# Other priorities in the first stage of a transformer-trunk kernel: gating columns ahead of a latent block, gate products and norm statistics first on VectorE

## The chip, the cores and the metric

The kernel runs on one core of one Trainium2 chip. The metric is the device time of one execution in microseconds (us); the time given is the median of some runs. In the profile PE is the tensor engine (PEld its weight loads, which overlap), DVE is VectorE, ACT is ScalarE, POOL is GpSimd, SP is SyncE, which issues most DMAs here.

## What is computed

One layer of a decoder trunk over 1024 tokens of width 1024, in float32. The input is RMS-normalized and multiplied by one input projection, whose columns feed four groups of heads; each group's output (width 256) is RMS-normalized, and all go through one output projection and are added to the residual. A squared-ReLU MLP of width 4096 and a last RMSNorm follow.

```
z = rms_norm(h, mix_norm_g[l]) @ w_in[l]
z_conv, z_mla, z_pool, z_gmlp = jnp.split(z, split_at, axis=-1)
...
# conv_module: y = a * sigmoid(g); causal depthwise convolution with 31 taps;
y = jax.nn.silu(layer_norm(y, ln_g, ln_b))
return y @ pw_w
...
# spatial_gating: v = rms_norm(v); chunks of 128 tokens, 4 heads
gate = jnp.einsum('hij,bnjhd->bnihd', ws * causal, v) + bs.T[None, None, :, :, None]
return u * gate.reshape(b, s, GROUP_WIDTH)
...
h = h + mixed @ w_out[l]
f = jnp.square(jax.nn.relu(rms_norm(h, ffn_norm_g[l]) @ w_ff1[l]))
h = h + f @ w_ff2[l]
```

"Latent" columns are those of the latent attention (z_mla, 352 columns), "gating" columns those of the spatial gating (z_gmlp, 512 columns).

## The kernel before

Every float32 matmul is done as three passes over a high and a low part (`mm3`, L160): ScalarE writes the rounded high part, VectorE (or GpSimd) the difference, the low part (`split`, L131 to L133; `split_scaled`, L135 to L137). Tokens are handled in two halves of 512 (`hf`) and eight tiles of 128.

The first stage, to about 400 us, holds everything up to the MLP. `z_mm(name, hf, jp)` (L421) projects the gating columns ("zgm") or the latent ones ("zml") of two token tiles: 48 matmuls into one `X` tile of PSUM (two such tiles exist), over four weight slices `zgm0` to `zgm3` or `zml0` to `zml3`. Each slice is loaded and split by `z_load`. Then the tile is read by `evac_gmlp` (ScalarE copies and squares, L441 to L443, a power on GpSimd, a scaling on VectorE, L446) or by `evac_mla` (ScalarE L457 to L459, small copies on GpSimd, scalings on VectorE, L463 and L464). `gmlp` (L501) multiplies the gating weights with the normalized half (gate matmuls, L510), then VectorE forms the products `ug` (L515: gate plus bias, times u), and PE transposes them (`ogT`, L521). The convolution (`conv_even_odd`, L353) is a chain of about 30 taps for each of two channel halves on VectorE (L351); its sum is `acc`. `conv_ln(u)` (L557) does the layer norm for a quarter of the tokens: four PE transposes into the one `K` bank of PSUM (`lnb`, L562), statistics (L567), aggregation (L568), a power on GpSimd, normalization (`yn`, L572), and four transposes back (`lnT`, L577). `wo_tile` multiplies a group's output with the output projection and adds it to the residual `h` (L495, "residual sum").

Up to the MLP the order of the work isn't written out. The kernel is traced in program order, and when it is built a planner runs through it on a clock of its own estimates: whenever an engine is free, it gives it the ready instruction with the lowest rank. The rank is the position in the program; inside `tc.high_priority(offset=n)` it is that position less n. The result is one fixed queue for each engine; on the chip each engine takes its queue in order and waits where an operand isn't there. Offsets of 2000 and 4000 reach ahead of everything that is traced up to there; an offset of 1 is nearly none. Tiles of one tag (`X`, `K`) were handed out in program order in the run before. The MLP from about 400 us on is ordered by hand (`run`, L905), and the planner doesn't touch it.

The part of the program text that the change touches stands in this order: `z_mm("zgm", 1, 0)`; `z_mm("zml", 1, 1)` at 4000; `gmlp(0)`; weights of the output projection at 300; `z_mm("zml", 0, 0)` at 2000; `z_mm("zml", 0, 1)`; `gmlp(1)`; `z_mm("zml", 1, 0)`; pooling; the convolution; `conv_ln(0)`, and between other work `conv_ln(1)` to `conv_ln(3)`.

Of the kernel before, what the change touches and what calls it, by code (L numbers as in the profile page):

```python
# [12 lines left out]
ALU = mybir.AluOpType  # L13
# [14 lines left out]
GW = 256  # L28
# [21 lines left out]
C_BS = 19  # L50
# [12 lines left out]
def trunk_kernel(tc, a):  # L63
    nc = tc.nc
    act = nc.scalar
    dve = nc.vector
    pool = nc.gpsimd
    pe = nc.tensor
    with (
        tc.tile_pool(name="sb", bufs=1) as sb,  # L70
        tc.tile_pool(name="ps", bufs=1, space=bass.MemoryType.PSUM) as ps,
        tc.tile_pool(name="hbm", bufs=1, space=bass.MemoryType.DRAM) as hbm,
    ):
        _trunk(tc, nc, act, dve, pool, pe, sb, ps, hbm, a)


def _trunk(tc, nc, act, dve, pool, pe, sb, ps, hbm, a):
# [4 lines left out]
    def const(shape, name, dt=F32):  # L82
        return sb.tile(shape, dt, tag=name, name=name)
# [6 lines left out]
    def pair(tag, name, shape):  # L90
        return [U(tag, name + "_h", shape, F32R), U(tag, name + "_l", shape, F32R)]
# [14 lines left out]
    def M(name, shape):  # L106
        return sb.tile([P] + shape, F32, tag="M", name=name, bufs=NM)
# [7 lines left out]
    def small(n, name, bufs=2):  # L115
        return sb.tile([P, n], F32, tag=name, name=name, bufs=bufs)

    def X(name):
        return ps.tile([P, 1024], F32, tag="X", name=name, bufs=2)

    def W(name):
        return ps.tile([P, 512], F32, tag="W", name=name, bufs=2)

    def K(name):
        return ps.tile([P, 512], F32, tag="K", name=name, bufs=1)

    def O(name):
        return ps.tile([P, 512], F32, tag="O", name=name, bufs=1)


    def split(h, l, src):  # L131
        act.activation(h, src, AF.Copy)
        dve.tensor_sub(l, src, h.bitcast(F32))  # L133
# [30 lines left out]
    def power(out, ssq, n, name, scale, expo):  # L164
        ms = small(n, name + "_ms")
        pool.tensor_scalar(ms, ssq, scale, EPS, ALU.mult, ALU.add)
        pool.tensor_tensor(out, ms, expo[:, :n], ALU.pow)

    def rstd(ssq, n, name, scale=1.0):
        rs = small(n, name + "_rs")  # L170
        power(rs, ssq, n, name, scale, nhalf)
        return rs


    cols = const([P, NCOL], "cols")
# [91 lines left out]
    b = X("zc")  # L267
# [56 lines left out]
    for i, hf in ((1, 0), (0, 1), (1, 1)):  # L324
        if (i, hf) == (0, 1):
            ba, bg = K("zc"), O("zc")
        else:
            b = X("zc")
# [46 lines left out]
    for i in range(2):  # L375
        w = load_w(a["w_cm"][4 + i], 1024, "wp%d" % i)
        b = X("zp")
# [43 lines left out]
    def z_mm(name, hf, jp):  # L421
        width, evac = {"zgm": (512, evac_gmlp), "zml": (352, evac_mla)}[name]
        b = X(name)
        for s in range(4):
            for j in range(2):
                lo = (2 * jp + j) * P
                for kk in range(2):
                    k = 2 * s + kk
                    mm3(b[:, j * 512:j * 512 + width], lambda x: xk(hf, k, x, lo, lo + P),
                        lambda y: wz[name, s][:, y, kk * width:(kk + 1) * width], k == 0, k == KD - 1)  # L430
        for j in range(2):
            evac(hf, 2 * jp + j, b[:, j * 512:(j + 1) * 512])
# [68 lines left out]
    def gmlp_chain(hf, wst):  # L501
        vs = pair("O", "gv", [4, GW])
        split(vs[0], vs[1], vg[hf])
        og = ug[hf]
        for hp in range(2):
            b = W("gate")
            for j in range(2):
                hd = 2 * hp + j
                for i, (x, y) in enumerate(PASSES):
                    pe.matmul(b[:, j * GW:(j + 1) * GW], wst[:, x, hd * P:(hd + 1) * P],  # L510
                              vs[y][:, :, hd * 64:(hd + 1) * 64], start=i == 0, stop=i == 2)
            for j in range(2):
                hd = 2 * hp + j
                og_h = og[:, :, hd * 64:(hd + 1) * 64]
                dve.scalar_tensor_tensor(og_h, b[:, j * GW:(j + 1) * GW].rearrange("p (n c) -> p n c", n=4),  # L515
                                         cols[:, C_BS + hd:C_BS + hd + 1], og_h, ALU.add, ALU.mult)
        oT = pair("OP"[hf], "oTg", [2, 512])
        for ct in range(2):
            b = W("ogT")
            for j in range(4):  # L520
                pe.transpose(b[:, j * P:(j + 1) * P], og[:, j, ct * P:(ct + 1) * P], ident)  # L521
            split(oT[0][:, ct, :], oT[1][:, ct, :], b)
        ssq = small(4, "ogs")
        jk = M("ogj", [GW])
        for j in range(4):
            act.activation(jk, og[:, j, :], AF.Square, accum_out=ssq[:, j:j + 1])
        return oT, rstd(ssq, 4, "ogr", 1.0 / GW)
# [29 lines left out]
    def conv_ln(u):  # L557
        hf = u // 2
        b = K("lnb")
        for j in range(2):  # L560
            for ct in range(2):
                pe.transpose(b[:, j * GW + ct * P:j * GW + (ct + 1) * P],  # L562
                             acc[ct][:, j, u * P:(u + 1) * P], ident)
        st = small(12, "bst", 1)
        mv = small(4, "bmv", 2)
        for j in range(2):
            dve.bn_stats(st[:, 6 * j:6 * j + 6], b[:, j * GW:(j + 1) * GW])  # L567
            dve.bn_aggr(mv[:, 2 * j:2 * j + 2], st[:, 6 * j:6 * j + 6])  # L568
        rs = rstd(mv.rearrange("p (j c) -> p j c", c=2)[:, :, 1], 2, "lnr")
        yn = M("yn", [2 * GW])  # L570
        for j in range(2):
            dve.tensor_scalar(yn[:, j * GW:(j + 1) * GW], b[:, j * GW:(j + 1) * GW], mv[:, 2 * j:2 * j + 1],  # L572
                              rs[:, j:j + 1], ALU.subtract, ALU.mult)
        b = O("lnT")
        for ct in range(2):
            for j in range(2):
                pe.transpose(b[:, ct * GW + j * P:ct * GW + (j + 1) * P], yn[:, j * GW + ct * P:j * GW + (ct + 1) * P],  # L577
                             ident)
        vh = M("vh", [2, GW])
        for ct in range(2):  # L580
            act.activation(vh[:, ct, :].rearrange("p (n c) -> p c n", c=2),
                           b[:, ct * GW:(ct + 1) * GW].rearrange("p (c n) -> p c n", c=2), AF.Identity, scale=lnhalf[:, ct:ct + 1],
                           bias=lnhalf[:, 2 + ct:3 + ct])
        th = M("th2", [2, GW])
        act.activation(th, vh, AF.Tanh)
        dve.scalar_tensor_tensor(vh, th, 1.0, vh, ALU.add, ALU.mult)
        if u % 2 == 0:
            us[hf] = pair("BP"[hf], "us%d" % hf, [2, 512])
        sl = slice((u % 2) * GW, (u % 2 + 1) * GW)
        split(us[hf][0][:, :, sl], us[hf][1][:, :, sl], vh)  # L590
# [713 lines left out]
    def gmlp(hf):  # L1304
        outs[3, hf] = gmlp_chain(hf, wst)
# [28 lines left out]
    with tc.high_priority(offset=1000):  # L1334
        load_wo(3, 1, pool)
    z_mm("zgm", 1, 0)
    with tc.high_priority(offset=4000):
        z_mm("zml", 1, 1)
    gmlp(0)
    with tc.high_priority(offset=300):  # L1340
# [18 lines left out]
    with tc.high_priority(offset=300):  # L1359
        wo_tile(3, 0, 3)  # L1360
        wo_tile(3, 0, 1)
    conv_ln(0)
    latent_T(0)
    with tc.high_priority(offset=300):
        load_h(4)
    outs[2, 1] = pool_chain(1, pw)
    conv_ln(1)
    wo_tile(3, 0, 0)
    load_h(5)
    load_wo(0, 1, pool)  # L1370
    wo_tile(3, 1, 1)
    conv_ln(2)
    with tc.high_priority(offset=300):
        wo_tile(2, 0, 2)
# [303 lines left out]
```

## Time and profile before

| | |
|---|---|
| median of 3 runs | 1024.47 us (1022.46 to 1025.44) |
| profiled execution | 1026.12 us, its span 1024.4 us |
| busy, PE / DVE / ACT / POOL | 993.5 / 822.5 / 500.8 / 206.1 us |
| mean granted PE clock | 0.988 |

The span is the time from the first to the last instruction of the profiled execution. In a row of the list in order of time stand start, duration, engine, line, operation, output<-inputs, shapes and count; in brackets the idle time of the engine just before, and what ended it. In a row of the list of waits stand the total, the count and the longest. In a row of the windows stand the window, its length, then each engine's busy time, the granted PE clock, and the DMAs' share and rate.

### The profile page before, as it was taken

The page shows a single profiled execution, that of the slowest core. Times are in us where ns is not written, and L with a number is a line of the kernel's source. Part 1 is how long each engine was busy: PE and PEld are TensorE (multiplying, and loading weights), DVE is VectorE, ACT ScalarE, POOL GpSimd, SP SyncE. Part 2 cuts the span into 40 slices and gives each one's busy share as a digit, 9 for nine tenths or more (in the row PEclk, how much of TensorE's full clock was granted, in tenths as well). Part 3 has the DMA queues.
Part 4 walks back from the last instruction along what each step waited for, and adds up shares of the span by engine and source line. Part 5 has one row for each costly group of instructions (what it writes and reads, how often), then busy time and mean ns, then how long its engine had stood idle before and what let it go on. Part 6 is the DMA issues. An engine that isn't in the chain of part 4 may idle for free.

```text
span 1024.4 us, 13323 instructions
## 1 busy us (share of the span) xinstructions
PE 993.5 (97%) x4674; PEld 818.5 (80%) x4674; DVE 822.5 (80%) x1275; ACT 500.8 (49%) x932; POOL 206.1 (20%) x304
## 2 busy tenths in 40 slices
PE   9999898989999999999999999999999999999996
PEld 7888697868888887878888887888688888888885
DVE  5899999977888666777776666558988888988997
ACT  7622355545667768774455554543341431431435
POOL 0037275213232312231121211211000000000004
PEclk9999999989999999999999999999999999999999
DMA  9521043011002006876766674559677067168004
GB/s 333 222 76 35 21 149 109 1 52 42 1 1 83 1 1 250 289 293 226 246 226 225 220 248 168 217 213 414 279 256 283 36 237 291 48 210 303 0 1 165
DMA packets 49348, 165.71 MB, mean 162 GB/s; under 512 B 6016, under 2 KB 7680, under 8 KB 49280
## 3 DMA queue, kind: packets, MB, share of 16 engines
q1 hardware_dynamic: 36000, 119.42, 33.2%
q0 software_dynamic: 12992, 45.10, 11.3%
q8 instruction: 37, 0.61, 0.3%
q10 hardware_dynamic: 288, 0.33, 0.1%
q14 instruction: 31, 0.25, 0.1%
HBM read 113.45 MB, written 51.38 MB: 161 GB/s over the span
## 4 chain that ended last, share of the span: by engine, by line
PE 68%; DVE 11%; issue 7%; DMA 6%; ACT 4%; POOL 3%; SPq 0%; POOLq 0%; DVEq 0%; ACTq 0%
PE ffb L162 15%; PE ffx L162 13%; PE ffa L162 11%; PE ffy L162 8%; PE wo L162 5%; PE ffe L162 4%; DVE acc L351 3%; PE ob L162 2%; PE s L698 2%; DMA raw_b<-in_w_ff 1%; DMA raw_f<-fr 1%; PE ptb L741 1%; PE woa L162 1%; DMA wcm_raw<-in_w_cm 1%; DVE h L495 1%
## 5 line engine op out<-in xcount | busy, mean ns | idle before, releaser
L162 PE MATMUL ffb<-wop,fop 128*128 128x512 f32 x756 | 179.3, 396 | 2.3 <-ACT wop L900 1.6
L162 PEld LDWEIGHTS ffb<-wop,fop 128*128 128x128 f32 x756 | 141.8, 188 | 37.7 <-ACT wop L900 2.4
L162 PE MATMUL ffx<-hnT,wop 128*128 128x512 f32 x624 | 149.5, 392 | 0.9 <-DVE s L963 0.8
L903 DVE TENSOR_TENSOR wop<-w_raw,wop 128x512 fp32r<-128x512 f32 x112 | 76.2, 689 | 78.5 <-ACT wop L900 78.3
L162 PEld LDWEIGHTS ffx<-hnT,wop 128*128 128x128 f32 x624 | 117.0, 188 | 27.7 <-DVE s L963 1.2
L162 PE MATMUL ffa<-wop,fop 128*128 128x512 f32 x576 | 135.1, 393 | 0.0
L162 PEld LDWEIGHTS ffa<-wop,fop 128*128 128x128 f32 x576 | 108.2, 188 | 25.0
L900 ACT ACTIVATE wop<-raw_b 128x512 fp32r<-128x512 f32 x96 | 59.6, 623 | 116.2 <-PE ffa L162 38.4
L900 ACT ACTIVATE wop<-w_raw 128x512 fp32r<-128x512 f32 x112 | 68.7, 625 | 42.5 <-DVE w_raw L1043 18.9
L900 ACT ACTIVATE fop<-raw_f 128x512 fp32r<-128x512 f32 x64 | 39.9, 623 | 80.2 <-DVE h_back L1099 27.6
L903 DVE TENSOR_TENSOR wop<-raw_b,wop 128x512 fp32r<-128x512 f32 x96 | 65.6, 683 | 5.8 <-ACT wop L900 5.3
L162 PE MATMUL ffe<-hnT,wop 128*128 128x512 f32 x288 | 68.7, 395 | 0.7 <-ACT m L996 0.7
L1279 POOL TENSOR_SCALAR mr_ms<-mssq,epsr 128x1 f32<-128x1 f32 x6 | 4.5, 752 | 297.4 <-ACT fjunk L1272 297.4
L162 PEld LDWEIGHTS ffe<-hnT,wop 128*128 128x128 f32 x288 | 53.5, 188 | 12.7 <-ACT m L996 1.2
L162 PE MATMUL ffy<-hnB,wop 128*128 128x512 f32 x192 | 46.9, 393 | 0.4 <-ACT s L996 0.4
L162 PE MATMUL ffy<-hnT,wop 128*128 128x512 f32 x192 | 46.5, 391 | 0.0
L974 POOL DMA_DIRECT2D fs<-fst x48 | 25.9, 539 | 90.1 <-DVE fst L133 86.7
L903 DVE TENSOR_TENSOR fop<-raw_f,fop 128x512 fp32r<-128x512 f32 x64 | 43.8, 685 | 0.0
L162 PEld LDWEIGHTS ffy<-hnB,wop 128*128 128x128 f32 x192 | 36.0, 188 | 9.0 <-ACT s L996 0.9
L162 PEld LDWEIGHTS ffy<-hnT,wop 128*128 128x128 f32 x192 | 36.1, 188 | 8.0
L721 POOL TENSOR_SCALAR P<-P,rr 128x384 f32<-128x384 f32 (+7 forms) x32 | 24.6, 768 | 47.8 <-DVE rr L720 47.5
L698 PE MATMUL s<-kb,qT 128*128 128x512 f32 (+2 forms) x144 | 32.9, 360 | 0.8 <-DVE h L495 0.8
(462 smaller groups left out, 2169.5 us busy)
## 6 DMA issues: line engine op xcount, KB each, us to landing
fs<-fst POOLq DMA_DIRECT2D x48, 512.0 KB, 3.3
fop<-fs SPq DMA_DIRECT2D x48, 512.0 KB, 7.7
w_raw<-in_w_ff SPq DMA_DIRECT2D x44, 512.0 KB, 4.3
raw_b<-in_w_ff SPq DMA_DIRECT2D x32, 512.0 KB, 5.4
raw_f<-fr SPq DMA_DIRECT2D x32, 512.0 KB, 5.3
fr<-s POOLq DMA_DIRECT2D x32, 256.0 KB, 3.2
fr<-f POOLq DMA_DIRECT2D x20, 256.0 KB, 2.4
xin<-in_x SPq DMA_DIRECT2D x8, 512.0 KB, 8.4
```

The lines of the kernel that those rows point to most:

```text
L162: pe.matmul(out, lhs(x), rhs(y), start=start and i == 0, stop=stop and i == 2, skip_group_check=more)
L351: dve.scalar_tensor_tensor(out[:, k:], src[:, 0:512 - k], c, out[:, k:], ALU.mult, ALU.add)
L495: dve.scalar_tensor_tensor(h[t], b, rs, h[t], ALU.mult, ALU.add)
L698: pe.matmul(sb_[:, c0:c0 + w], q[:, x, qo:qo + P], kt[:, y, 0:w], start=i == 0, stop=i == 2 and not last)
L721: pool.tensor_scalar(pt, pt, rr, 1.0, ALU.mult, ALU.mult)
L741: pe.transpose(b[:, place[j] + s * P:place[j] + (s + 1) * P], pts[s][:, (2 * kp + j) * P:(2 * kp + j + 1) * P], ident)
L900: act.activation(self.t[:, 0], self.src(), AF.Copy)
L903: dve.tensor_sub(self.t[:, 1], self.src(), high(self.t))
L974: pool.dma_start(fs[p][q], t.rearrange("p x c -> p (x c)").bitcast(F32))
L1279: eng.tensor_scalar(ms, fin["ssq", t], epsr[:, t:t + 1], 1.0, ALU.add, ALU.mult)
```

## The change

Three places get other priorities; no instruction is added or removed. The latent block of tiles 6 and 7 loses its offset of 4000 (1 is left), the gate products and all VectorE and GpSimd work of a norm quarter up to the normalization get 4000, and the four transposes of a norm quarter are traced with the second channel half first.

```diff
@@ gmlp_chain
             for j in range(2):
                 hd = 2 * hp + j
                 og_h = og[:, :, hd * 64:(hd + 1) * 64]
-                dve.scalar_tensor_tensor(og_h, b[:, j * GW:(j + 1) * GW].rearrange("p (n c) -> p n c", n=4),
-                                         cols[:, C_BS + hd:C_BS + hd + 1], og_h, ALU.add, ALU.mult)
+                with tc.high_priority(offset=4000):
+                    dve.scalar_tensor_tensor(og_h, b[:, j * GW:(j + 1) * GW].rearrange("p (n c) -> p n c", n=4),
+                                             cols[:, C_BS + hd:C_BS + hd + 1], og_h, ALU.add, ALU.mult)
@@ conv_ln
-        for j in range(2):
-            for ct in range(2):
+        for ct in (1, 0):
+            for j in range(2):
                 pe.transpose(b[:, j * GW + ct * P:j * GW + (ct + 1) * P],
                              acc[ct][:, j, u * P:(u + 1) * P], ident)
-        st = small(12, "bst", 1)
...
+        with tc.high_priority(offset=4000):
+            st = small(12, "bst", 1)
+            mv = small(4, "bmv", 2)
+            for j in range(2):
+                dve.bn_stats(st[:, 6 * j:6 * j + 6], b[:, j * GW:(j + 1) * GW])
+                dve.bn_aggr(mv[:, 2 * j:2 * j + 2], st[:, 6 * j:6 * j + 6])
+            rs = rstd(mv.rearrange("p (j c) -> p j c", c=2)[:, :, 1], 2, "lnr")
+            yn = M("yn", [2 * GW])
+            for j in range(2):
+                dve.tensor_scalar(yn[:, j * GW:(j + 1) * GW], b[:, j * GW:(j + 1) * GW], mv[:, 2 * j:2 * j + 1],
+                                  rs[:, j:j + 1], ALU.subtract, ALU.mult)
@@ the program text
     z_mm("zgm", 1, 0)
-    with tc.high_priority(offset=4000):
+    with tc.high_priority(offset=1):
         z_mm("zml", 1, 1)
     gmlp(0)
```

More of the change, by code (lines that the diff above doesn't have):

```diff
@@ L559, in conv_ln @@
         b = K("lnb")
-        for j in range(2):
-            for ct in range(2):
+        for ct in (1, 0):
+            for j in range(2):
                 pe.transpose(b[:, j * GW + ct * P:j * GW + (ct + 1) * P],
                              acc[ct][:, j, u * P:(u + 1) * P], ident)
-        st = small(12, "bst", 1)
[L565 to L573, printed above, removed]
+        with tc.high_priority(offset=4000):
[9 more added lines that the diff above has]
+                                  rs[:, j:j + 1], ALU.subtract, ALU.mult)
         b = O("lnT")
```

## The prediction

> **What bounds the kernel now.** I read the page first, then the list of waits for the tensor engine (PE), then a table of time windows, then the instructions in order of time around each hole. The page:
>
> ```profile
> span 1024.4 us, 13323 instructions
> PE 993.5 (97%) x4674; PEld 818.5 (80%) x4674; DVE 822.5 (80%) x1275; ACT 500.8 (49%) x932; POOL 206.1 (20%) x304
> DVE  5899999977888666777776666558988888988997
> PEclk9999999989999999999999999999999999999999
> ```
>
> PE is busy for 993.5 of 1024.4 us, so a gain can only come from the 31 us in which it is not, or from busy time at a lower clock. VectorE (DVE) has 80% over the span, but in its slices 2 to 8 (26 to 205 us) stand an 8 and six 9s: it is full in the stage that the change touches. What PE waits for, the largest rows that lie in this stage:
>
> ```profile
> PE ogT L521 <- DVE ug L515: 3.3, 2, 2.8
> PE zml L162 <- ACT zgm L443: 3.0, 1, 3.0
> PE lnT L577 <- DVE yn L572: 2.5, 1, 2.5
> PE zml L162 <- DVE zml0l L133: 0.9, 1, 0.9
> PE zml L162 <- DVE zml3l L133: 0.8, 1, 0.8
> ```
>
> These are 3.3 + 3.0 + 2.5 + 0.9 + 0.8 = 10.5 us. The windows show what comes with them (busy time of each engine, then the granted clock under PEclk):
>
> ```profile
> 75.00:164.00 89.00, 80.98 (x419) 71.20 (x418) 86.31 (x129) 35.78 (x92) 51.89 (x55) 0.97 0.24 81
> 118.30:121.60 3.30, 2.81 (x7) 2.33 (x8) 2.58 (x5) 2.16 (x4) 3.05 (x4) 0.50 0.00 0
> 123.50:159.80 36.30, 34.98 (x223) 34.32 (x224) 34.50 (x58) 18.04 (x53) 23.71 (x31) 1.00 0.45 157
> 162.70:165.90 3.20, 2.79 (x10) 2.33 (x11) 3.16 (x7) 1.89 (x4) 2.90 (x5) 0.50 0.56 172
> 220.70:234.20 13.50, 12.33 (x34) 9.37 (x35) 7.57 (x13) 6.47 (x12) 2.19 (x2) 0.50 0.00 0
> 234.80:400.00 165.20, 162.20 (x983) 139.55 (x983) 125.47 (x215) 111.10 (x221) 48.90 (x78) 1.00 0.11 35
> ```
>
> From 75 to 164 us DVE is busy for 86.31 of 89 us: there it sets the pace, and PE waits. In three places PE runs at half clock, for at least 3.3, 3.2 and 13.5 us. At full clock this work takes half as long, so the three cost about 1.6, 1.6 and up to 6.7 us. After 234.8 us PE is busy for 162.20 of 165.20 us at full clock, so there is little to win there and something to lose. The three holes, with their clock, are worth about 3.0 + 1.6, 2.8 + 1.6 and 2.5 + 6.7 = 18 us: the ceiling of the change.
>
> **The latent block moved back (4000 to 1).** No instruction is added. The 48 matmuls of this block, its reads of the bank on ScalarE, four small POOL copies, the POOL powers and four DVE scalings lose their lead; it issues no DMA, so SP's queue is passed by nothing. Around it:
>
> ```profile
> 115.35 0.40 PE L162 MATMUL zgm<-zgm3h,xT_l 128*128 128x512 f32 x1
> 118.79 0.66 PE L162 MATMUL zml<-zml0h,xT_h 128*128 128x352 f32 x1 [3.04 <-ACT zgm L443]
> ...
> 122.21 0.40 PE L162 MATMUL zgm<-zgm3h,xT_l 128*128 128x512 f32 x1
> 123.55 0.43 PE L162 MATMUL zml<-zml0l,xT_h 128*128 128x352 f32 x1 [0.95 <-DVE zml0l L133]
> ...
> 130.69 0.43 PE L162 MATMUL zml<-zml3l,xT_h 128*128 128x352 f32 x1 [0.76 <-DVE zml3l L133]
> ```
> ```profile
> 122.61 0.89 DVE L133 TENSOR_TENSOR zml0l<-zml_raw,zml0h 128x704 fp32r<-128x704 f32 x1
> ```
>
> PE's queue holds the first latent matmul ahead of the last nine gating ones. It waits 3.04 us for a bank that ScalarE still reads; then the nine run; then PE waits 0.95 us for zml0l. With the change the nine run in the hole, from 115.6 to about 117.7 (nine at the pitch of 0.23 us that the starts before the hole have). But the second latent matmul still needs zml0l, which VectorE writes at 122.61 to 123.50, behind convolution taps that this edit doesn't move. So by 123.55 PE has done exactly the same work: value 0. Two ends. Below nothing: a block of offset 2000 that follows can now overtake the moved one, and its first three quarters cover the 0.76 us before 130.69: -0.8. Above: the holes merge into one of about 5.4 us (0.9 ahead of the one latent matmul, 4.4 behind it), and by the rows above 3.04 us idle was enough for a stretch of half clock; two such stretches from 121.6 on would cost half of the 5 us that lie after 123.55, +2.5. That is less than the 2.77 us that PE idles at 163.12 below, so I keep 0.
>
> **The gate products first on DVE.** Eight instructions change rank; none is added.
>
> ```profile
> 157.01 0.28 PE L510 MATMUL gate<-gv_h,wst 128*128 128x256 f32 x1
> 163.12 1.94 PE L521 MATMUL ogT<-ident,ug 128*128 128x128 f32 x8 [2.77 <-DVE ug L515]
> ```
> ```profile
> 153.67 1.21 DVE L133 TENSOR_TENSOR gv_l<-vg,gv_h 128x1024 fp32r<-128x1024 f32 x1
> ...
> 160.25 1.28 DVE L137 SCALAR_TENSOR_TENSOR wo_0l<-wo_raw,cols,wo_0h 128x1024 fp32r<-128x1024 f32 x1
> 161.45 0.73 DVE L351 SCALAR_TENSOR_TENSOR acc<-ycv,hsum,acc 128x502 f32<-128x502 f32 x1
> 162.10 1.65 DVE L515 SCALAR_TENSOR_TENSOR ug<-gate,cols,ug 128x256 f32<-128x256 f32 x4
> ```
>
> The products (L515) start at 162.10, though the gate matmuls end at 157.29: 4.8 us that a first rank could win. But the tap just ahead (161.45) is written later in the program than the products, so it ranked lower already, and still went first. So the planner's own clock did not hold the products ready; a higher rank doesn't help an instruction that the planner thinks is not ready. Value 0; the other end is the whole hole and its half clock, -(2.8 + 1.6) = -4.4. No end above nothing: what they could push back is taps, which have slack until the first norm at 172.13. I take 0 as the nearer, by the tap at 161.45.
>
> **The norm statistics first on DVE, and the transposes' order.** Four units of two statistics, two aggregates and two normalizations on DVE and two small POOL operations move up; no DMA, so SP's queue is passed by nothing, and POOL sat idle before the small operations anyway:
>
> ```profile
> POOL lnr_ms L166 <- DVE bmv L568: 22.3, 3, 12.6
> ```
>
> The 16 transposes into the bank stay 16, in another order; both statistics start together once the bank is full (172.13), and would after: 0. First and last unit, and the cost of a projection tile:
>
> ```profile
> 172.13 0.76 DVE L567 BATCH_NORM_STATS2 bst<-lnb 128x6 f32<-128x256 f32 x2
> ...
> 178.26 0.99 DVE L572 TENSOR_SCALAR yn<-lnb,bmv,lnr_rs 128x256 f32<-128x256 f32 x2
> ...
> 216.16 0.75 DVE L137 SCALAR_TENSOR_TENSOR cT<-ctb,cols,cT 128x512 fp32r<-128x512 f32 x1
> 216.83 1.27 DVE L495 SCALAR_TENSOR_TENSOR h<-wo,cr_cr,h 128x1024 f32<-128x1024 f32 x1
> 218.02 0.75 DVE L567 BATCH_NORM_STATS2 bst<-lnb 128x6 f32<-128x256 f32 x2
> ...
> 218.77 0.66 DVE L133 TENSOR_TENSOR oTc_l<-pwc,oTc_h 128x512 fp32r<-128x512 f32 x1
> 219.35 0.17 DVE L568 BATCH_NORM_AGGREGATE bmv<-bst 128x2 f32<-128x6 f32 x1
> ...
> 220.62 1.00 DVE L572 TENSOR_SCALAR yn<-lnb,bmv,lnr_rs 128x256 f32<-128x256 f32 x2 [0.53 <-POOL lnr_rs L167]
> ```
> ```profile
> 218.30 0.39 PE L162 MATMUL pwc<-us_h,cw 128*128 128x512 f32 x1
> 221.22 1.36 PE L577 MATMUL lnT<-ident,yn 128*128 128x128 f32 x4 [2.53 <-DVE yn L572]
> ```
> ```profile
> 235.68 2.75 PE wo L162 x12
> ```
>
> In the first unit 6.1 us pass from statistics to normalization (172.13 to 178.26), with residual sums (L495) between. Rank can take out some 3 us, but PE is full of projection matmuls there: 0. In the last unit PE has nothing else: its hole from 218.69 to 221.22 is this chain. One residual sum (216.83, 1.27 us, next start 1.19 us later) goes ahead of the statistics; it is the one piece in which rank can matter. The copy at 218.77 ranked lower and still went, so it fills a gap that rank doesn't close; so does the POOL power (219.52 to 220.62). I take -1.2; the ends are 0 (the statistics were not ready either) and -2.5 (the hole goes).
>
> **The half clock behind the last norm.** With 1.2 us less the hole is 1.3 us. Nearest rows: 0.95 us (before 123.55) was followed by full clock (the window from 123.5), 2.53, 2.77 and 3.04 us by half clock. 1.3 lies nearest to 0.95, so the 13.5 us at half clock go. PE was busy for 12.33 of them, and would need 6.2; but DVE has 7.57 us of work in the same stretch, partly in line with PE, so I let it shrink to about 9: -4.5, with ends 0 and -6.2. By the Trainium skill (TensorE: Matmul & The Clock Gate, Part 1) a gate halves the clock after at least one idle window of about 3.4 us. The length of the stretches agrees (3.3, 3.2, and 13.5 as four), the threshold does not: holes of 2.5 to 3.0 us were enough here.
>
> **What can be pushed back.** Statistics (0.94 us a unit from 218.02 to about 218.96 if nothing lies between) and normalizations (0.99 us) now go ahead of residual sums. A projection tile takes PE 2.75 us, and its sum 1.27 us, in two banks: 1.5 us of cover. Should the statistics stand in DVE's queue before the bank is full, everything behind them waits too, sums and splits. Value 0; if it goes, 4 units by 0.4 us, and up to three stretches of half clock.
>
> **Sum.** 0 + 0 - 1.2 - 4.5 = -5.7 us. The profiled execution took 1026.12 us (span 1024.4 and 1.7 around it), 1.65 us more than the median of the runs, 1024.47. Against its own time that is 1020.4; against the median, 1018.8 us.
>
> **The rivals.** First, nothing that counts moves: VectorE's order is set by what the planner held ready, the last norm keeps its place, and PE's order moves with it. Speaks for it: the taps at 161.45 and the copy at 218.77, both of lower rank and both first. Against: the sum at 216.83. Time 1024.5, give or take 3. In this case the change doesn't do what it says.
>
> Second, a special form of it, on the clock. If the 13.5 us at half clock were not set off by the hole but by what PE did in them (four transposes, then matmuls with breaks), they stay when it shrinks: only -1.2, 1023.3 us. Against it: half clock follows all three holes of 2.53 to 3.04 us. The Trainium skill's page on TensorE, by the rule given above, would have it this way, since no hole here is a whole window.
>
> Third, slower: the norms come ahead of the residual sums and the banks come free late. It decides once a sum ends more than 1.5 us late, and 0.94 + 0.99 us put ahead of one sum pass that by 0.4. Four units make 1.7 us of holes, and if each of two or three brings a stretch of half clock at 1.6 us, or the one at 220.7 stays and another comes, 4 us more: about +6, 1030.5 us. The planner works every later order out anew, and the 165 us after 234.8 have only 3 us of idle to lose to, which makes new holes likelier than fewer.
>
> Fourth, faster still: the products also pass the weight split at 160.25 and the taps around it, and the second hole goes: 1018.8 - 4.4 = 1014.4 us.
>
> **How the numbers follow.** Forecast 0.36, fourth 0.11, first 0.21, second 0.05, third 0.27. Faster by over 0.3% (3.1 us, about what a measurement can tell here) is 0.36 + 0.11 = 0.47, the same 0.26, slower 0.27. The range goes from the fourth's time less some of the first edit's and the last norm's other ends (-0.8, -1.3, -1.7), 1011, to the third's, 1030. The forecast's own range is 1015 to 1021.
>
> **What would show it.** Right: a hole before lnT L577 under 1.5 us and full clock in the 15 us after it; zml0l still the wait of the first latent block, with gating matmuls ahead of its first one; products at the old distance from the gate matmuls, and the ogT hole at 2 to 3 us. Wrong: half clock after lnT as before, PE waits on residual sums L495 between 165 and 218 us, or new holes after 235 us.

## The result, and the profile after

The kernel after takes 1030.94 us (median of 4 runs, 1030.73 to 1031.68), the kernel before 1024.95 us beside it (4 runs, 1022.46 to 1026.56). The ratio is 1.0063, with a 95% interval of 1.0046 to 1.0080: the change costs some 6 us, where 5.7 us of gain were forecast. The profiled execution after took 1031.14 us.

The page of the kernel after, the lines that answer to those of before:

```profile
span 1029.4 us, 13322 instructions
PE 993.0 (96%) x4674; PEld 817.8 (79%) x4674; DVE 824.2 (80%) x1275; ACT 501.3 (49%) x932; POOL 211.1 (21%) x304
PEclk9999999999999999999999999999999999999998
```

PE is busy for 993.0 us, as before (993.5); the span is 5 us longer. So the loss is time in which PE does nothing. Where it lies is seen from the time windows of the kernel after (PE, PEld, DVE, ACT and POOL busy, then the granted clock), and for comparison those of a run that has the queues of before (e3, below):

```profile
75.00:164.00 89.00, 82.67 (x422) 73.33 (x422) 86.01 (x128) 36.58 (x98) 55.12 (x56) 0.96 0.22 76
164.00:200.00 36.00, 32.82 (x164) 26.54 (x162) 31.62 (x50) 15.17 (x30) 11.83 (x16) 1.00 0.15 50
200.00:235.00 35.00, 28.08 (x136) 22.07 (x135) 30.25 (x45) 18.83 (x32) 7.99 (x8) 0.97 0.12 38
235.00:400.00 165.00, 162.00 (x974) 139.22 (x974) 124.02 (x213) 110.35 (x219) 47.84 (x76) 1.00 0.09 28
```

```profile
75.00:164.00 89.00, 82.45 (x418) 72.14 (x416) 86.33 (x127) 35.54 (x91) 52.19 (x56) 0.96 0.23 81
164.00:200.00 36.00, 35.97 (x171) 30.07 (x171) 33.26 (x58) 18.04 (x41) 10.38 (x18) 0.91 0.10 35
200.00:235.00 35.00, 31.52 (x152) 25.24 (x151) 29.18 (x42) 19.58 (x32) 7.74 (x7) 0.95 0.11 38
235.00:400.00 165.00, 162.00 (x979) 139.24 (x978) 125.75 (x216) 111.87 (x223) 48.22 (x78) 1.00 0.12 41
```

In the stage of the edit, up to 164 us, PE is as busy as in e3, and from 235 us on the two are alike (162.00 of 165 us). From 164 to 235 us PE has 32.82 + 28.08 = 60.9 of 71 us instead of 35.97 + 31.52 = 67.5: 6.6 us of holes more. The higher clock there (1.00 and 0.97 for 0.91 and 0.95) gives back about half of that. What PE waits for from 164 to 235 us in the kernel after:

```profile
PE wo L162 <- DVE h L495: 2.1, 2, 1.6
PE wo L162 <- ACT oTp_h L136: 1.6, 1, 1.6
PE wo L162 <- DVE oTg_l L133: 1.6, 2, 1.3
PE qb L162 <- ACT vh L583: 1.2, 1, 1.2
PE ctb L611 <- DVE cT L137: 1.2, 1, 1.2
PE pwc L162 <- ACT us_h L132: 1.1, 1, 1.1
```

No wait is longer than 1.6 us. The two long ones of before in this neighbourhood, ogT (2.77 us) and lnT (2.53 us), are both gone: small waits have taken their place. The place that the edit touches, in PE's order of time:

```profile
120.66 0.43 PE L162 MATMUL zml<-zml0h,xT_h 128*128 128x352 f32 x1 [0.78 <-ACT zgm L443]
125.41 0.66 PE L162 MATMUL zml<-zml0l,xT_h 128*128 128x352 f32 x1 [4.33 <-DVE zml0l L133]
125.87 0.49 PE L162 MATMUL zml<-zml0h,xT_l 128*128 128x352 f32 x1
126.16 0.41 PE L510 MATMUL gate<-gv_h,wst 128*128 128x256 f32 x1
```

The nine gating matmuls now run ahead, and the two waits (3.04 and 0.95 us before) have become 0.78 and 4.33 us, with a single matmul between. Behind them the gate matmuls (L510) of the first half stand between the latent ones. Before, three of them came ahead of the block's last quarter (from 129.42 us) and the rest behind the block.

One more thing has to be known before any number is compared. Run e3 has every queue in the order of before, but its trace has other stretches of half clock:

```profile
119.00:125.80 6.80, 5.81 (x14) 4.41 (x15) 6.08 (x11) 2.39 (x5) 4.13 (x4) 0.50 0.07 8
163.40:170.20 6.80, 6.17 (x18) 4.96 (x19) 6.73 (x13) 5.32 (x20) 4.24 (x7) 0.50 0.34 119
224.80:228.20 3.40, 3.40 (x10) 2.30 (x9) 2.00 (x4) 2.40 (x4) 2.42 (x2) 0.51 0.00 0
```

The same three holes are followed by 6.8, 6.8 and 3.4 us at half clock here, by 3.3, 3.2 and 13.5 us in the profile shown before. Behind the last hole the stretch differs by 10 us between two executions of the same queues, which is 5 us of matmul work.

### The profile page after: what moved, and what is told of

It reads as the page before. It is cut to its first block, busy times and chain, and to the rows that moved or that the text cites. A ratio compares the mean times of both kernels' runs of the same rounds, so it can differ in the third digit from the quotient of the medians.

```text
span 1029.4 us, 13322 instructions
## 1 busy us (share of the span) xinstructions
PE 993.0 (96%) x4674; PEld 817.8 (79%) x4674; DVE 824.2 (80%) x1275; ACT 501.3 (49%) x932; POOL 211.1 (21%) x304
## 4 chain that ended last, share of the span: by engine, by line
PE 46%; issue 25%; DVE 10%; POOL 8%; DMA 6%; ACT 4%; SPq 0%; POOLq 0%; DVEq 0%; ACTq 0%
PE ffb L162 15%; PE ffa L162 11%; PE wo L162 4%; PE ffe L162 4%; DVE acc L351 3%; POOL fr L961 3%; PE ob L162 2%; PE s L700 2%; POOL fs L976 2%; DMA xraw<-in_xT 2%; DMA raw_f<-fr 2%; PE ptb L743 1%; PE woa L162 1%; DVE h L495 1%; DMA fop<-fs 1%
```

## The experiments

Beside each result stands its ratio to runs of the kernel before on the same chip, with the 95% interval; 0.001 is 1 us. The order of instructions that is spoken of is that of the built kernels, engine by engine. A tie (`issue_after`, `behind`) fixes which of two pieces of work the planner puts first. Of each edit the lines that matter are shown, in short form.

**Which part of the change.** e1 has the latent edit alone, e2 the transposes' order alone, e3 the ranks of products and statistics, e4 is the change once more.

```
e1:  -    with tc.high_priority(offset=4000):
     +    with tc.high_priority(offset=1):
              z_mm("zml", 1, 1)
e2:  -    for j in range(2):
     -        for ct in range(2):
     +    for ct in (1, 0):
     +        for j in range(2):
e3:  +    with tc.high_priority(offset=4000):   # products (L515); statistics and yn (L567 to L572)
```

> Only the latent block's offset goes from 4000 to 1; products, norms and transposes stay as before. Theory A (the whole loss comes from the latent block: its first matmul still waits for zml0l, now in one long hole with half clock behind it, and everything behind it is ordered anew): +5 to +7 us, about 1031, with the 4.3 us hole before zml0l. Theory B (the transposes' order costs it, since the statistics of the first quarter come later): within 2 us of before. Theory C (neither; the gate and norm ranks matter): within 2 us of before.

> Only the order of the four transposes of a norm quarter changes. Theory A: within 2 us of before. Theory B: +4 us or more. The queues differ from before in some 27 places on PE, 10 on VectorE, all between 159 and 215 us, so if anything a hole moves there; half clock behind the last norm may stay or go (up to 5 us faster).

> Only the gate products and the norm work get offset 4000. The queues of all five engines come out the same as before, instruction for instruction, so theories A and B expect the time of before within 1 us (1024 to 1026). It is also a second profile of the program before: if the clock at the start, between 5 and 12 us, or around 725 us differs from before's profile, those are chance and not the change. Theory C: slower by 4 us or more.

> The changed kernel once more. Its time again 1030 to 1032. Its first profile began the gating matmuls 2.0 us later than before, and had half clock at 8 to 11 us and at 728 to 731 us, none of which the change touches. If these are chance, this profile places them elsewhere and the time spreads by some 2 us; if they belong to the changed program, they are here again.

Measured: e1 1029.34 us (1.0044, 1.0031 to 1.0057), e2 1024.94 (1.0009, 0.9997 to 1.0021), e3 1023.96 (1.0001, 0.9988 to 1.0013), e4 1029.41 (1.0053, 1.0040 to 1.0066). The latent edit alone makes 4.4 of the 5.3 us that e4 shows, and the intervals overlap; the other edits make nothing that is clear of noise. The two rank edits do not move one instruction on any engine; put on top of the latent edit, the products' rank swaps one product with one scaling. In the kernel after a residual sum still stands ahead of the statistics, although it ranks lower:

```profile
177.68 1.28 DVE L495 SCALAR_TENSOR_TENSOR h<-wo,ogr_rs,h 128x1024 f32<-128x1024 f32 x1
178.87 0.75 DVE L569 BATCH_NORM_STATS2 bst<-lnb 128x6 f32<-128x256 f32 x2
```

The profile of the kernel after has two stretches of 3.4 us at half clock far from the edit, at 8 and at 728 us. The profile of e4, the same kernel, has neither, so they are chance; e4 is 1.5 us below the first measurement.

**The merged wait, or what follows it.** e5 keeps rank 4000 and ties the latent block behind the last gating matmul: 7 lines of PE's order move. e6 takes the 4.3 us wait out of the kernel after. e7 and e8 have the latent edit, and hold back one of the two things that it lets pass: the first half's gate matmuls, or the other half's latent block.

```
e5:  +    with tc.high_priority(offset=4000), tc.issue_after(last_zgm):
              z_mm("zml", 1, 1)
e6:  +    ss = (1, 0, 2, 3) if name == "zml" else range(4)
     -    for s in range(4):
     +    for s in ss:
e7:  +    with tc.issue_after(last_zml):
              gmlp(0)
e8:  +    with tc.high_priority(offset=2000), tc.issue_after(last_zml):
              z_mm("zml", 0, 0)
```

> The kernel before, rank 4000 kept, but the latent block is tied behind the last gating matmul on the tensor engine: the nine gating matmuls run ahead of the first latent one, and nothing else of the queues moves (7 lines of PE's order, 3 of VectorE's). Theory D, the merged wait costs it: one hole of about 5 us ahead of the second latent matmul, half clock behind it for 7 us, and most of the loss is here: 1027 to 1030 us. Theory E, what follows in the re-planned order costs it (gate matmuls between the latent ones, a later block that overtakes, the norms later): the hole is there and costs nothing, since VectorE sets the pace up to 164 us: 1023.5 to 1025.5 us, and 3.5 us of holes from 164 to 235 us as before.

> The kernel after, but each latent block takes its weight slices in the order 1, 0, 2, 3. Slice 1 has its low part long before slice 0, so the wait of 4.3 us for zml0l ahead of the second latent matmul should shrink to under 1.5 us; VectorE's order is that of the kernel after. Theory D: the loss goes with the hole, 1024 to 1026 us. Theory E: what PE gains there it waits later, since VectorE's work is the same: 1028 to 1030 us, with about 10 us of holes from 164 to 235 us as in the kernel after.

> The kernel before with the latent block at rank 1, and the gate matmuls of the first half (L510) tied behind the last matmul of that block, as the old rank had them; the block of offset 2000 (zml of the other half) may still overtake. Theory D: hole of 4 to 5 us, 1027 to 1030 us. Theory E in the form that the gate matmuls between the latent ones (and with them the products and transposes that come early and the first norm that comes late) cost it: 1024 to 1026 us. Theory E in the form that the overtaking block costs it: 1028 to 1030 us.

> The kernel before with the latent block at rank 1, and the block of offset 2000 (zml of the other half) tied behind its last matmul, so that it can't overtake; the gate matmuls may still go between the latent ones. Theory D: hole of 4 to 5 us, 1027 to 1030 us. Theory E, gates form: 1028 to 1030 us. Theory E, overtaking form: 1024 to 1026 us.

Measured: e5 1025.21 us (1.0013, 1.0002 to 1.0023), e6 1029.38 (1.0055, 1.0042 to 1.0067), e7 1028.05 (1.0037, 1.0023 to 1.0050), e8 1029.54 (1.0055, 1.0042 to 1.0069). Theory D falls from both sides. The merged wait without the rest costs about 1.3 us. In e6 the wait for zml0l shrank to 1.08 us while the time stayed, because a later latent block then waited for a bank that ScalarE still read:

```profile
130.84 0.66 PE L162 MATMUL zml<-zml1h,xT_h 128*128 128x352 f32 x1 [4.42 <-ACT zgm L444]
```

In the kernel after VectorE is busy for 86.01 of the 89 us there, and e6 has its order: what PE gains it waits later. Of theory E neither form was right: holding back one of the two brings at most a third back.

**Both held back.** e11 has the ties of e7 and e8 together.

> The kernel before with the latent block at rank 1, and both the gate matmuls of the first half and the block of offset 2000 tied behind its last matmul. That gives PE nearly the order of the run with the nine gating matmuls first and nothing else moved (25 lines differ). Theory E, the loss is what the lower rank lets move ahead of the block: it goes, 1024 to 1026.5 us, though neither tie alone brought it. Rival, that the block itself is late (its reads on ScalarE, its small POOL operations): 1028 to 1030 us.

Measured: 1024.37 us (0.9997, 0.9984 to 1.0011). The loss is gone, though the latent block has rank 1 and the nine gating matmuls run first. Its waits show the hole of the kernel after beside the last norm of before:

```profile
PE zml L162 <- DVE zml0l L133: 4.3, 1, 4.3
PE lnT L579 <- DVE yn L574: 2.5, 1, 2.5
```

So a hole of over 4 us with half clock behind it costs little (1.3 us in e5, nothing here), and the loss comes with what the lower rank lets pass the block: either of the two is enough for most of it.

**A longer tap.** In the kernel after POOL's split of wq runs beside convolution taps, in the kernel before beside the gate products:

```profile
167.57 2.77 POOL L150 TENSOR_TENSOR wql<-wq_raw,wqh 128x1024 fp32r<-128x1024 f32 x1 [1.70 <-ACT wqh L149]
168.62 3.03 DVE L351 SCALAR_TENSOR_TENSOR acc<-ycv,hsum,acc 128x499 f32<-128x499 f32 x2
```

```profile
161.88 2.52 POOL L150 TENSOR_TENSOR wql<-wq_raw,wqh 128x1024 fp32r<-128x1024 f32 x1 [2.85 <-ACT wqh L149]
```

Two taps beside it take 3.03 us; alone one takes 0.73. The four products beside it (162.10, quoted in the prediction) took 1.65 us, 0.48 each, which is what one takes elsewhere. e9 and e10 let POOL write an eighth of wql and leave out the rest of the low part, with all queues unchanged:

```
     +    m = P if name == "wq" else n
     -    sub.tensor_sub(w[:, 1, :n], raw[:, :n], w[:, 0, :n].bitcast(F32))
     +    sub.tensor_sub(w[:, 1, :m], raw[:, :m], w[:, 0, :m].bitcast(F32))
...
     -    lambda x: wq[:, x, kt * 512 + hd * P:kt * 512 + (hd + 1) * P]
     +    lambda x: wq[:, 1, :P] if x else wq[:, 0, kt * 512 + hd * P:kt * 512 + (hd + 1) * P]
```

> The kernel after with every queue in its order, but POOL's split of wq (L150, wql, 2.77 us) writes 128 columns instead of 1024, and the matmuls that read wql read these 128 columns each time; the query projection's low part is left wrong by that. In the trace of the kernel after, a convolution tap on VectorE that runs beside this split takes 2.26 us instead of 0.73. Theory P, this stall is part of the loss: the tap takes 0.73 us, VectorE's work up to the first score is 1.5 us shorter, and the time is 1 to 2 us below the kernel after: 1027.5 to 1028.5 us. Rival: VectorE waits as long elsewhere, the time stays at 1029 to 1030 us.

> The same edit in the kernel before, again with every queue in its order. There the split ran beside the gate products, which read a PSUM bank and took 0.48 us each, as elsewhere. Theory P: nothing to win, within 0.7 us of the kernel before. Rival, that the split's end itself is waited for: 1 to 2 us faster.

Measured: e9 1028.23 us (1.0047, 1.0032 to 1.0062), e10 1023.84 (0.9997, 0.9987 to 1.0006). The pair of taps fell to 1.50 us:

```profile
166.10 0.86 POOL L151 TENSOR_TENSOR wql<-wq_raw,wqh 128x128 fp32r<-128x128 f32 x1 [1.68 <-ACT wqh L149]
167.17 1.50 DVE L352 SCALAR_TENSOR_TENSOR acc<-ycv,hsum,acc 128x499 f32<-128x499 f32 x2
```

The 1.5 us of VectorE's time are shown. What they are worth in time, 0.6 us by the two ratios (1.0053 to 1.0047), is less than the intervals can tell from nothing.

**Two other splits on VectorE.** e12 changes load_wo(3, 1, pool) and load_wo(0, 1, pool) to dve in the kernel before.

> The kernel before with two weight splits (wo of group 3, half 1, and of group 0, half 1) on VectorE in place of POOL. In the trace of before they stall a tap to 2.89 us and another split to 2.56 us, 2.15 and 1.9 us over what these take alone; on VectorE each costs 1.28 us, so VectorE has 1.5 us less. It also gives ScalarE one pass less for each. Theory P: 1022 to 1023.5 us if the order stays as good; PE's queue differs in 126 lines from before, and by what the runs with a re-planned order showed that can cost 4 us: then 1027 to 1029 us.

Measured: 1028.44 us (1.0043, 1.0026 to 1.0060). This edit has nothing to do with the latent block. It gives VectorE two splits of 1.28 us and takes two stalls of about 2 us from it, moves 126 lines of PE's order, and costs 4 us as well.

**The last norm, 90 us behind the edit.** In the kernels after, e1, e4, e6, e7, e8, e9 and e12 the last norm's transposes stand ahead of the output tiles wo_tile(2, 1, 3) and wo_tile(2, 1, 2), 24 matmuls; in before, e2, e5, e10 and e11 they stand behind them. All of the first group cost 3.7 to 6.3 us, none of the second more than 1.3. PE in e3 (order of before), then in the kernel after:

```profile
216.89 0.60 PE L563 MATMUL lnb<-ident,acc 128*128 128x128 f32 x4
217.25 0.48 PE L162 MATMUL pwc<-us_h,cw 128*128 128x512 f32 x1
...
222.66 1.00 PE L579 MATMUL lnT<-ident,yn 128*128 128x128 f32 x4 [2.41 <-DVE yn L574]
```

```profile
214.39 0.60 PE L563 MATMUL lnb<-ident,acc 128*128 128x128 f32 x4
...
216.58 0.63 PE L611 MATMUL ctb<-ident,zmla 128*128 128x128 f32 x4 [1.16 <-DVE cT L137]
217.68 0.50 PE L162 MATMUL wo<-wo_0h,oTp_h 128*128 128x512 f32 x1 [0.47 <-DVE h L495]
...
228.28 0.74 PE L162 MATMUL qb<-cT,wqh 128*128 128x512 f32 x2 [1.20 <-ACT vh L583]
230.35 1.05 PE L481 MATMUL ssqb<-ones,ss 128*128 128x2 f32 x8 [0.41 <-DVE ss L540]
232.46 0.50 PE L162 MATMUL pwc<-us_h,cw 128*128 128x512 f32 x1 [1.05 <-ACT us_h L132]
233.33 1.19 PE L162 MATMUL kb<-cT,wkvh 128*128 128x512 f32 x2 [0.37 <-DVE cr_cm L483]
```

e13 and e14 give the kernel after the old order there, e15 and e16 give the kernel before the new one, by ties alone (lnb: the four transposes of conv_ln(3); ctb: those of latent_T(1); w: wo_tile; behind(a, b) puts b behind a). They move 7, 24, 13 and 13 lines of PE's order against the kernel that they start from.

```
e13:  after  + behind(w[2,1,2], lnb)
e14:  after  + behind(ctb[:4], w[2,1,1]); behind(ctb, w[2,1,3] and w[2,1,2]); behind(w[2,1,2], lnb)
e15:  before + behind(lnb, w[2,1,3] and w[2,1,2])
e16:  before + behind(w[2,1,1], ctb)
```

> The kernel after, with the four transposes of the last norm (lnb, conv_ln(3)) tied behind the two output tiles of group 2 (24 wo matmuls) ahead of which the kernel before doesn't have them either; 7 lines of PE's order and 16 of VectorE's move. Theory T, the order at 200 to 240 us costs it: 1024.5 to 1027 us, and the waits of ctb and qb there shrink. Rival U, the loss is made in the stage of the edit and only shows there: 1028 to 1030 us.

> As the run before, and the first four transposes of the second half's latent columns (ctb, latent_T(1)) stand ahead of the output tile wo_tile(2, 1, 1), as in the kernel before. Theory T: 1023.5 to 1026 us. Rival U: 1028 to 1030 us.

> The kernel before, with the last norm's four transposes ahead of the two output tiles of group 2, as in the kernel after; 13 lines of PE's order and 18 of VectorE's move. Theory T: 1 to 4 us slower than before, 1025.5 to 1028.5 us. Rival U: 1023.5 to 1025 us.

> The kernel before, with the second half's latent transposes behind wo_tile(2, 1, 1), as in the kernel after; the last norm's transposes stay behind the two output tiles. Theory T: 1 to 4 us slower than before, 1025.5 to 1028.5 us. Rival U: 1023.5 to 1025 us.

Measured: e13 1027.84 us (1.0038, 1.0024 to 1.0053), e14 1027.96 (1.0038, 1.0023 to 1.0054), e15 1026.57 (1.0025, 1.0015 to 1.0034), e16 1023.44 (0.9995, 0.9985 to 1.0005). Theory T holds in part: with 13 lines of PE's order e15 makes the kernel before 2.5 us slower, while e16, which moves the latent transposes, makes no difference. The trace of e15 shows how:

```profile
212.46 0.63 PE L562 MATMUL lnb<-ident,acc 128*128 128x128 f32 x4 [1.99 <-DVE vt_l L133]
...
223.43 0.74 PE L162 MATMUL qb<-cT,wqh 128*128 128x512 f32 x2 [1.20 <-ACT vh L581]
225.50 1.05 PE L481 MATMUL ssqb<-ones,ss 128*128 128x2 f32 x8 [0.41 <-DVE ss L539]
227.60 0.50 PE L162 MATMUL pwc<-us_h,cw 128*128 128x512 f32 x1 [1.05 <-ACT us_h L132]
228.47 0.86 PE L162 MATMUL kb<-cT,wkvh 128*128 128x512 f32 x2 [0.37 <-DVE cr_cm L483]
```

These are the waits of the kernel after one for one: 1.20, 0.41, 1.05 and 0.37 us. The early norm takes away the 2.4 us before lnT, brings 3.0 us in four pieces behind it, and a wait of 2.0 us ahead of it, as its bank is still being read. In the kernel after the old order there brings only about 1.5 us back (1.0053 to 1.0038), which the intervals can't tell from nothing, and no more with the latent transposes put back too. Most of the loss, 3.8 of 5.3 us, stays with the old tail.

**Do the prices add up?** e17 is e14 with the narrow split of e9; e18 is e15 with the tie of e5.

> The kernel after with the old order of the tail (the last norm's transposes behind two output tiles, the second half's first latent transposes ahead of another) and POOL's split of wq narrowed to 128 columns (the query projection's low part is left wrong by that). If the prices add up: 1029.4 - 1.5 - 1.2 = 1026.7 us, and what is left of the loss is the hole's 1.3 and a remainder of about 1.5. If they cover the same time: 1027.5 to 1028.5 us.

> The kernel before with the nine gating matmuls ahead of the latent block (rank 4000 kept) and the last norm's transposes ahead of the two output tiles. If the prices add up: 1024 + 1.3 + 2.5 = 1027.8 us, most of the loss of the change with 20 lines of PE's order moved instead of 179. If they cover the same time: 1026 to 1027 us.

Measured: e17 1028.37 us (1.0037, 1.0024 to 1.0051), e18 1028.11 (1.0024, 1.0009 to 1.0039; the before of its job 1024.79). By their middles neither adds up: the narrow split brings nothing once the tail is put back (3.7 us for 3.8 in e14), and hole and norm together cost what the norm costs alone (2.4 us for 2.5). But the sums, 3.8 us for e18 and 2.6 us for e17, lie within the intervals (0.9 to 3.9 and 2.4 to 5.1), so this is not decided.

The ledger of PE from its first gating matmul to its first score matmul, in single profiled executions. Holes are summed over all idle times of PE, up to 204 us of the span and behind, half clock is the length of the stretches, and the rest is the time less the holes and less half of the half clock:

| run | time, us | holes to 204 us | holes behind | half clock | rest |
|---|---|---|---|---|---|
| profile of before | 161.9 | 8.6 | 3.2 | 20.5 | 139.8 |
| e3 (same queues) | 158.5 | 6.9 | 3.2 | 17.1 | 139.9 |
| e11 (both held back) | 159.7 | 8.8 | 3.4 | 13.7 | 140.6 |
| e15 (before, norm ahead) | 159.6 | 7.8 | 5.0 | 10.2 | 141.6 |
| e7 (gates held back) | 161.9 | 8.7 | 5.7 | 13.7 | 140.7 |
| e8 (other half held back) | 163.1 | 9.6 | 5.7 | 13.7 | 140.9 |
| e14 (after, old tail) | 162.3 | 11.3 | 4.3 | 10.2 | 141.6 |
| e9 (after, narrow split) | 162.4 | 11.3 | 5.0 | 10.2 | 140.9 |
| kernel after | 163.3 | 11.1 | 5.3 | 10.2 | 141.8 |

From e3 to the kernel after: 6.3 us more holes, 3.5 us less by the clock, 1.9 us in the rest, together 4.8. These are single executions: the two of the same queues, before and e3, differ by 3.4 us themselves. No version beat both kernels: e10, e11 and e16 are within their intervals of the kernel before.

The ledger and the lists of waits also tell the two passing pieces apart. What e7 and e8 both have more than e11 lies behind 204 us, 5.7 us of holes for 3.4: both have the early norm and its four waits. From 164 to 207 us e7, whose gate matmuls are held back, has lost the waits for oTg_l and for h of the kernel after, and e8, whose gate matmuls pass, has them (e7 first):

```profile
PE wo L162 <- ACT oTg_h L132: 0.7, 1, 0.7
PE wo L162 <- ACT oTp_h L136: 0.4, 1, 0.4
```

```profile
PE wo L162 <- DVE h L497: 2.6, 2, 1.9
PE wo L162 <- DVE oTg_l L133: 1.3, 1, 1.3
PE wo L162 <- ACT oTp_h L136: 1.1, 1, 1.1
```

So the long ones of these waits come with the passing gate matmuls; e11 has 1.1 us for oTg_l and 0.6 us for h, in pieces under 0.8 us. They are worth little in sum: e7 keeps 2.3 us of the wait for ogT instead, and PE's holes from 155 to 204 us are 3.6 us in e7, 3.8 in e11, 4.3 in e8 and 4.7 in the kernel after.

## Why the prediction was wrong, by its steps

**The latent block moved back, 0.** This is the step that failed. Its picture of the place was right: nine matmuls ahead, a hole of 5.1 us (0.78 + 4.33, where 5.4 were expected), half clock behind it, and no more than its upper end of 2.5 us for that (e5: 1.3). It failed in that it priced only the block that goes back, and of what then goes ahead it named the block of offset 2000 alone, as a gain of up to 0.8 us. Held against the runs, letting that block pass costs 3.7 us (e7) and letting the gate matmuls pass, which the step doesn't mention, 5.5 us (e8). The two prices overlap: both together cost 4.4 us (e1), and nothing when both are held back (e11).

**The gate products first, 0, and the norm statistics first, -1.2.** The first is right and for the reason given: the planner didn't hold them ready, and rank moved nothing. The same reasoning, with the copy at 218.77 as its witness, stood in the second step and was overruled there by one row, the sum at 216.83. e3 shows 0 for both, which is the first rival's case as far as the ranks go. The transposes' order was put at 0, and e2 agrees (1.0009, 0.9997 to 1.0021).

**The half clock behind the last norm, -4.5.** Wrong in size: it was taken from one execution. Behind this hole, of 2.4 to 2.5 us each time, the stretch was 13.7 us in the profile of before and in e5, 6.8 in e11 and 3.4 in e3, which has the queues of before. So 4.5 us could be won against that one execution, not against the median of the kernel. The hole did go with the change, but because its transposes come earlier on PE (214.39 us for 216.89), not because rank took a sum out of VectorE's chain. The clock did give something back: half clock in the ledger fell from 20.5 (before) or 17.1 us (e3) to 10.2, which is 5.2 or 3.5 us, but 4.6 or 6.3 us of new holes took more.

**What can be pushed back, 0, and the third rival, 1030.5.** The rival had the time (1030.5 us, though the prediction's range ended at 1030), and its second reason, that every later order is worked out anew and makes new holes likelier than fewer, is what happened. Its mechanism was not: the rank put no norm ahead of a residual sum (e3). That its time agrees is luck as far as the mechanism goes. It looked for the new holes behind 235 us, where there are none; they lie from 164 to 235 us, of 0.4 to 1.6 us each. Of the signs named for a wrong prediction, PE's waits on L495 came (2.1 us); half clock right behind lnT did not, only 3.4 us of it 7 us later, at 233.1 us. Two signs named for a right one came as well, though the time went the other way: no hole before lnT, and zml0l as the wait of the first latent block.

**The second rival, the clock.** By the Trainium skill (TensorE: Matmul & The Clock Gate, Part 1) the clock is halved after an idle window of about 3.4 us. The stretches in the ledger are 3.4 us or multiples of it (6.8, 13.7), which agrees. That shorter holes were enough does not: 2.4 to 3.0 us in before and e3, 1.55 us in e17. Whether the stretch behind the last norm hangs on the hole or on what PE does there the runs don't decide, as its length is chance.

What stays open: a full account of the 5.3 us by places. The runs fix the cause to the two passing pieces and to the orders that follow from letting them pass, and they price one later rearrangement on its own (2.5 us, e15). With that one put back in the kernel after, 3.8 us (2.3 to 5.4) remain, for which the waits above are a place but not a price. And e12 leaves a wider rival standing: that a larger rearrangement of this order, whatever starts it, costs some 4 us.

## What to carry to other kernels

Lowering one block's rank is an edit to everything that may now pass it: list what stands behind it in the queue, ties included, and price those; then expect the planner's later order to change too, here 90 us further on. Before building on a stretch of half clock, look at a second execution of the same kernel. When a rank edit is weighed, compare the built queues first: the two rank edits here moved nothing on their own.

## What the runs showed of the hardware

An elementwise instruction of VectorE with two SBUF inputs stood still while POOL subtracted two SBUF tensors. A tap of 0.73 us took 2.26 beside the split of wq, and 0.73 again when the split was cut to an eighth and had ended before it (e9). Products with one input in PSUM kept their 0.48 us beside the same split. The Trainium skill (SBUF — State Buffer, SBUF: two separate sides) tells of a port pair that the two engines hold in turn, and only for VectorE instructions with two SBUF inputs or in a 2-port mode; the taps and the products agree with it. A scaling with one SBUF tensor as input stood still too, in the kernel after beside POOL's split of wo; the same scaling takes 0.28 us at 163.07. Whether it ran in such a mode no view here shows.

```profile
160.50 2.42 DVE L463 TENSOR_SCALAR zmla<-zmla,mr_rs 128x128 f32<-128x128 f32 x1
```

The length of a hole alone doesn't tell whether half clock follows. In the kernel after, six holes of 0.5 to 1.6 us from 164 to 218 us passed at full clock; in e6 the last two of them (1.16 and 0.47 us) were followed by 3.4 us at half clock. A hole of 2.05 us in e7 (before 213.6 us) and one of 2.97 us in e10 passed at full clock up to the next hole, and one of 1.55 us in e17 (before 207.16 us) was followed by 3.4 us at half clock. e10's hole, with the window behind it:

```profile
118.43 0.43 PE L163 MATMUL zml<-zml0h,xT_h 128*128 128x352 f32 x1 [2.97 <-ACT zgm L444]
118.40:123.20 4.80, 2.54 (x11) 1.78 (x11) 4.08 (x8) 1.69 (x2) 3.43 (x4) 1.00 0.00 0
```

Short holes close together can do it as well: in the kernel after, three holes that made 2.7 us within 6 us (qb, ssqb and pwc above) and the start of a fourth (kb) had a stretch of 3.4 us at half clock behind them.
